# Expert matrices of a mixture layer loaded in rows of 4 KB instead of 2 KB

## The chip, the cores and the metric

The kernel runs on one core of a Trainium2 chip. The metric is the device time of one execution in microseconds (us). Before the change it was 2349.37 us, the median of three runs between 2348.11 and 2349.89 us. A number of loads or rows below is a count; 1 KB is 1024 bytes.

## The reference

Two blocks follow each other on 256 tokens of 1024 values, all in 32-bit floats. The first has two layers, and in its first layer 256 context tokens run beside. Each layer of it modulates and normalizes, attends (`mixer_ab`, then `mixer_c`), and ends in a mixture of 32 experts, of which each token takes two. The second block (two more layers of other attention and a dense feed-forward part) is not touched by the change. What matters here is the mixture:

```
h = rms_norm(x, norm_ffn[l]) * (1 + scale) + shift
pg = softmax(h @ w_group + b_group); le = h @ w_expert + b_expert    # group, then two experts of its eight
expert_block = lambda xb, e: (silu(xb @ w1[e]) * (xb @ w3[e])) @ w2[e]  # w1, w3: 1024 x 512; w2: 512 x 1024
out[token] = sum over its two experts of weight * expert_block(h[token], e)
```

One expert matrix is 2 MB, so a layer reads 32 x 3 x 2 MB = 192 MB (201.3 million bytes) of expert weights, whatever the tokens choose.

## The kernel before

One program runs on five engines: TensorE (PE) multiplies, VectorE (DVE) and ScalarE (ACT) work on rows, GpSimd (POOL) does small pieces, and SyncE (SP) issues nearly all loads. A scheduler of the compiler orders most instructions; `late` (line 185) and the order tokens on TensorE (`pe`, line 1019) hold the loads and the mixture's products in the order of the text.

The mixture (`moe`, line 997) takes the experts in 16 pairs. The two experts of a pair work side by side on TensorE, each on 64 of the 128 columns, so 64 token slots each. `up` (line 1225) multiplies the gathered inputs `xp` by `w1` and `w3` of a pair, k from 0 to 7 over the 1024 input values. `turn` transposes the hidden values to `gp`, and `down` (line 1253), one pair behind, multiplies by `w2`, k from 0 to 3 over the 512 hidden values, first for output columns 0 to 511 (n = 0), then for 512 to 1023. `weigh` scales its result `y`, `scatter` adds it to the tokens every second pair, and `gather` makes the inputs `xp` for the next two pairs out of a one-hot matrix `G` and the normalized tokens, which line 1035 splits in two parts `hi` and `lo`. In the first layer `gather` and `scatter` run over 512 tokens (NT = 4 tiles of 128), in the second over 256 (NT = 2).

Each load of an expert matrix brings 512 KB into one slot of 128 partitions x 1024 values, by `raws` (line 295). For `w1` and `w3` that is two blocks of 128 rows of 512 values: partition p gets row p of the one block and row p of the next. For `w2` it is two blocks of 128 half rows of 512 values. Either way a partition receives two runs of 2 KB from two places in memory:

```
in_=ap[k0 * P:(k0 + g) * P, :].rearrange("(k p) f -> p k f", p=P)     # g = 1024 // cols = 2
ws = self.raws([ew("w2", e)[:, n * 512:n * 512 + 512] for e in es_])   # once for each n
```

A layer has 384 such loads and 22 slots (first layer) or 31 slots (second); `slots` and the table `MJ` (line 84) say which memory they use and when. A slot is filled again when the products that read it are done. The names `raw`, `r`, `x`, `y`, `wh` and `wl` in the rows are such slots. The 96 loads of `w_mod` in the first attention part (`mod_group`, line 362, the first 16 of them ahead of everything else) also bring 512 KB each, but as one run of 4 KB per partition: 1024 neighbouring columns of one row.

At the start `setup` (line 136) loads constants, biases and norms as short rows, transposes them into columns (`colA`), and loads the tokens `x`; its temporary memory is used again by the first slots.

Of the kernel before, what the change touches and what calls it, by code (L numbers as in the profile page):

```python
# [8 lines left out]
F32 = mybir.dt.float32  # L9
# [3 lines left out]
AF = mybir.ActivationFunctionType  # L13
ALU = mybir.AluOpType
# [104 lines left out]
class Kern:  # L119
# [16 lines left out]
    def setup(self, tmp):  # L136
        nc, I = self.nc, self.I
        kept = COFF["kept"][1]
        self.cst = self.t(self.cp, [P, kept])
        o3 = COFF["causal"][0]  # L140
        more = self.t(tmp, [P, CONST.shape[1] - o3])
        rows = self.t(tmp, [P, 2, P])
        rc = self.t(tmp, [16, P])
        nc.sync.dma_start(out=rc[0:8, :], in_=I["c"].rearrange("o (k p) -> (o k) p", p=P))
        nc.sync.dma_start(out=rc[8:16, :], in_=I["c_ctx"].rearrange("(k p) -> k p", p=P))
        nc.scalar.dma_start(out=self.cst, in_=I["const"][:, 0:kept])
        nc.scalar.dma_start(out=more, in_=I["const"][:, o3:])
        nc.scalar.dma_start(out=rows[0:96, 0, :], in_=I["b_mod"].rearrange("l (k p) -> (l k) p", p=P))
        nc.scalar.dma_start(out=rows[96:112, 0, :], in_=I["norm_mix"].rearrange("l (k p) -> (l k) p", p=P))
        nc.scalar.dma_start(out=rows[112:128, 0, :], in_=I["norm_ffn"].rearrange("l (k p) -> (l k) p", p=P))  # L150
        self.x = [self.res(4 + i) for i in range(4)]
        for i in range(4):
            src = I["x"][0] if i < 2 else I["ctx"][0]
            nc.scalar.dma_start(out=self.x[i], in_=src[(i % 2) * P:(i % 2 + 1) * P, :])
        self.ident = self.c("ident")
        self.colC = self.t(self.cp, [P, 16])
        tp = self.P("tp")
        nc.tensor.transpose(tp[:, 0:16], rc, self.ident[:16, :16])
        nc.vector.tensor_copy(self.colC, tp[:, 0:16])
        self.colA = self.t(self.cp, [P, P])  # L160
        tp = self.P("tp")
        nc.tensor.transpose(tp[:, 0:P], rows[:, 0, :], self.ident)
        nc.vector.tensor_copy(self.colA, tp[:, 0:P])
        more = {nm: more[:, COFF[nm][0] - o3:COFF[nm][0] - o3 + P] for nm in ("causal", "anti", "tri")}
        self.ones = self.t(self.cp, [P, 1])
        nc.vector.memset(self.ones, 1.0)
        self.identb = self.t(self.cp, [P, P], BF)
        nc.vector.tensor_copy(self.identb, self.ident)
        self.causb4 = self.t(self.cp, [P, 4, P], BF)
        nc.vector.tensor_copy(self.causb4, more["causal"][:, None, :].to_broadcast([P, 4, P]))  # L170
        self.causb = self.causb4[:, 0]
        self.antib = self.t(self.cp, [P, P], BF)
        nc.vector.tensor_copy(self.antib, more["anti"])
        self.mhalf = self.c("mhalf")
        self.trib = self.t(self.cp, [P, P], BF)
        nc.vector.tensor_copy(self.trib, more["tri"])
        self.onesb = self.t(self.cp, [P, P], BF)
        nc.vector.memset(self.onesb, 1.0)
        self.rank = self.c("rank")
        self.modcol = self.t(self.cp, [P, 2, 48, 2])  # L180
        self.modA = self.t(self.cp, [P, 2, 2, KT, 2])

    def late(self, **kw):

        self.tc.keep_in_program_order(self.nc.sync.dma_start(**kw))

    def setup_small(self):

        nc, I = self.nc, self.I
        self.wr = self.t(self.cp, [P, 2, KT, 36])  # L190
        self.br = self.t(self.cp, [P, 2, 36])
        for l in range(2):
            self.late(out=self.wr[:, l, :, 0:4], in_=I["w_group"][l].rearrange("(k p) f -> p k f", p=P))
            self.late(out=self.wr[:, l, :, 4:36], in_=I["w_expert"][l].rearrange("(k p) f -> p k f", p=P))
            self.late(out=self.br[:, l, 0:4], in_=I["b_group"][l:l + 1, :].to_broadcast([P, 4]))
            self.late(out=self.br[:, l, 4:36], in_=I["b_expert"][l:l + 1, :].to_broadcast([P, 32]))

# [94 lines left out]
        pool, tag, bufs = e  # L292
        return self.t(pool, [P, 1024], dt, tag=tag, bufs=bufs)

    def raws(self, aps):

        nk, cols = aps[0].shape[0] // P, aps[0].shape[1]
        g = 1024 // cols
        out = [[] for _ in aps]
        for k0 in range(0, nk, g):  # L300
            for o, ap in zip(out, aps):
                raw = self.slot("raw", F32)
                self.late(out=raw.rearrange("p (k f) -> p k f", k=g),
                                       in_=ap[k0 * P:(k0 + g) * P, :].rearrange("(k p) f -> p k f", p=P))
                o += [raw[:, i * cols:(i + 1) * cols] for i in range(g)]
        return out

# [54 lines left out]
    def mod_group(self, l, q, tag):  # L362


        nc = self.nc
        acc = self.P(tag)[:, 0:512]
        for step in range(4):
            hf = step // 2
            for k in range(4 * (step % 2), 4 * (step % 2) + 4):
                c0 = 2048 * q + 1024 * hf  # L370
                w = self.raws([self.I["w_mod"][l][k * P:k * P + P, c0:c0 + 1024]])[0][0]
                for c in range(4):
                    m = nc.tensor.matmul(acc[32 * c:32 * c + 32, 256 * hf:256 * hf + 256], self.csf[:, k, :],
                                         w[:, 256 * c:256 * c + 256], start=(k == 0), stop=(k == KT - 1))
                    self.tc.stamp_issue_order_token(m.ins, "mod")
            if step < 3:
                yield
        m = self.slot("wh", F32)[:, 0:512]
        nc.scalar.activation(m, acc, AF.Copy)
        tp = self.P("tp")  # L380
        for j in range(4):
            nc.tensor.transpose(tp[:, j * P:(j + 1) * P], m[:, j * P:(j + 1) * P], self.ident)

        for hf in range(2):
            tv = tp[:, 256 * hf:256 * hf + 256].rearrange("p (j c s) -> p c j s", j=2, c=4)[:, :, :, 0:2]
            b0 = q * 16 + 8 * hf
            bias = self.colA[:, l * 48 + b0:l * 48 + b0 + 8].rearrange("p (c j) -> p c j", c=4)
            nc.vector.tensor_tensor(out=self.modcol[:, l, b0:b0 + 8, :].rearrange("p (c j) s -> p c j s", c=4), in0=tv,
                                    in1=bias[:, :, :, None].to_broadcast([P, 4, 2, 2]), op=ALU.add)
        if q != 1:  # L390
            which = q // 2
            g = self.colA[:, 96 + 16 * which + 8 * l:96 + 16 * which + 8 * l + 8]
            sc = self.modcol[:, l, 24 * which + 8:24 * which + 16, :]
            nc.vector.scalar_tensor_tensor(self.modA[:, l, which], sc, 1.0, g[:, :, None].to_broadcast([P, KT, 2]),
                                           op0=ALU.add, op1=ALU.mult)
        yield
# [572 lines left out]
    def logits(self, l, who, xt, t, tag, half):  # L969
# [4 lines left out]
        for b in range(2):  # L974
# [1 line left out]
            nc.scalar.activation(half(), xt[:, c], AF.Square, accum_out=ss[:, b:b + 1])  # L976
            tp = self.P("tp")
            for j in range(4):
                nc.tensor.transpose(tp[:, j * P:(j + 1) * P], xt[:, (4 * b + j) * P:(4 * b + j + 1) * P], self.ident)
            xT = half()  # L980
            if b == 0:
                nc.scalar.activation(xT, tp, AF.Copy)
# [14 lines left out]
    def moe(self, l, whos, ahead=list):  # L997
# [37 lines left out]
        xp_ = []  # L1035
        for i, x in enumerate(xs):
            hi, lo = (self.t(mp, [P, D], F32R) for _ in range(2))
            nc.scalar.activation(hi, x, AF.Copy, scale=rr_[:, i:i + 1])
            stt(lo, x, rr_[:, i:i + 1], hi.bitcast(F32), op0=ALU.mult, op1=ALU.subtract)
            xp_.append((hi, lo))  # L1040
        st = lambda *s, dt=F32, **kw: self.t(mp, [P, NT] + list(s), dt, **kw)
        big_ = lambda: self.t(mp, [P, 160], tag="big", bufs=1)
# [182 lines left out]
        def up(es_, xp, between=()):  # L1225
# [4 lines left out]
            for b, nm in enumerate(("w1", "w3")):  # L1230
                if b and between:
                    scatter(between)
                ws = self.raws([ew(nm, e) for e in es_])
                for k in range(KT):
                    for i, w in enumerate(ws):
                        c = slice(64 * i, 64 * i + 64)
                        mm(H[c, b, :], xp[:, k, c], w[k], start=(k == 0), stop=(k == KT - 1))
# [14 lines left out]

        def down(es_, gp):
            y = self.P("mm").rearrange("p (a b) -> p a b", a=2)
            for n in range(2):
                ws = self.raws([ew("w2", e)[:, n * 512:n * 512 + 512] for e in es_])
                for k in range(4):
                    for i, w in enumerate(ws):
                        c = slice(64 * i, 64 * i + 64)
                        mm(y[c, n, :], gp[:, k, c], w[k], start=(k == 0), stop=(k == 3))  # L1260
            return y[:64 * len(es_)]

        def weigh(y, tk, w):
# [701 lines left out]
```

## Time and profile before

| | |
|---|---|
| median of the runs | 2349.37 us |
| the profiled execution, its own time | 2353.45 us |
| its span, to which the rows refer | 2351.7 us |
| PE busy | 2181.2 us (93%) |
| DVE, ACT, POOL busy | 1119.8, 780.7, 345.9 us |
| bytes moved by DMA | 593.12 MB, 252 GB/s over the span |
| mixture of the first layer, about | 345 to 870 us |
| mixture of the second layer, about | 1119 to 1648 us |

The span is what lies between the first and the last instruction; the time of the run has 1.75 us around it. A busy PE counts a product from its start to its modelled end, with its place in the pipeline, so 93% does not say that TensorE had no time left. The DMA share can exceed 1, as neighbouring packets overlap a little in the records.

### The profile page before, as it was taken

How to read it: one execution, taken by the hardware profiler on the slowest of the kernel's cores; microseconds unless marked ns; L12 is line 12 of the kernel's file. 1: busy time of each engine (PE TensorE's matmuls, PEld its weight loads, DVE VectorE, ACT ScalarE, POOL GpSimd, SP SyncE). 2: the span in 40 equal slices, each digit the busy share in tenths (PEclk: the TensorE clock that was granted, in tenths of full speed). 3: DMA queues.
4: the chain of work that ended last, by engine and by line, in shares of the span. 5: the costliest groups of instructions: out<-in, count | busy, mean ns of one | idle time of the engine just before them, and what ended most of it. 6: DMA issues, size and time to landing. Idle time of an engine off the chain costs nothing. (4 is left out here: it accounts for less than half of the span.)

```text
span 2351.7 us, 32726 instructions
## 1 busy us (share of the span) xinstructions
PE 2181.2 (93%) x12405; PEld 1391.2 (59%) x12405; DVE 1119.8 (48%) x2251; ACT 780.7 (33%) x1585; POOL 345.9 (15%) x478
## 2 busy tenths in 40 slices
PE   5999989999999998998899999999899999899998
PEld 3865564444444437986433333333667998767997
DVE  4565664434343347766312122221566654666654
ACT  3444542111111115655201110110555443655443
POOL 1621120000000003443000000000323110232111
PEclk8999999999999999999899999999989999989999
DMA  8467639999999983220999999999433652425561
GB/s 290 134 226 270 220 113 367 381 387 387 387 387 386 387 303 114 77 72 9 357 387 387 386 387 387 386 387 383 152 126 116 230 178 99 160 84 169 188 207 37
DMA packets 306785, 593.12 MB, mean 252 GB/s; under 512 B 25270, under 2 KB 57020, under 8 KB 306620
## 3 DMA queue, kind: packets, MB, share of 16 engines
q1 hardware_dynamic: 305436, 587.68, 70.3%
q10 hardware_dynamic: 1184, 3.27, 0.4%
q8 instruction: 100, 1.64, 0.3%
q14 instruction: 65, 0.53, 0.1%
HBM read 589.82 MB, written 1.05 MB: 251 GB/s over the span
## 5 line engine op out<-in xcount | busy, mean ns | idle before, releaser
L330 POOL TENSOR_TENSOR wl<-raw,wh 128x1024 fp32r<-128x1024 f32 (+1 forms) x17 | 41.4, 2439 | 1148.8 <-SPq L1325 529.7
L1239 ACT ACTIVATE hs<-mm 128x512 f32<-128x512 f32 x32 | 19.1, 597 | 501.4 <-PE mm L1024 501.4
L330 DVE TENSOR_TENSOR wl<-raw,wh 128x1024 fp32r<-128x1024 f32 (+3 forms) x113 | 145.1, 1292 | 47.8 <-ACT wh L327 47.5
L1240 DVE TENSOR_TENSOR hs<-mm,hs 128x512 f32<-128x512 f32 x32 | 22.1, 691 | 297.6 <-ACT hs L1239 297.5
L1024 PE MATMUL mm<-x,xp 128*64 128x512 f32 x476 | 157.0, 601 | 4.7 <-DMA x<-in_w_dram 4.6
L1024 PE MATMUL mm<-raw,xp 128*64 128x512 f32 x464 | 149.4, 600 | 4.0 <-DMA raw<-in_w_dram 3.9
L327 ACT ACTIVATE wh<-raw 128x1024 fp32r<-128x1024 f32 (+3 forms) x113 | 115.8, 1032 | 84.2 <-PE pa L351 23.6
L1024 PE MATMUL mm<-r,xp 128*64 128x512 f32 x400 | 137.0, 601 | 4.1 <-DMA r<-in_w_dram 4.1
L1295 DVE TENSOR_TENSOR r<-tp,r 128x512 f32<-128x512 f32 x96 | 66.1, 690 | 102.3 <-PE tp L1024 102.1
L1250 ACT ACTIVATE gp<-tp 128x512 f32<-128x512 f32 x32 | 19.1, 597 | 264.4 <-PE tp L1248 264.4
L1024 PEld LDWEIGHTS tp<-G,u 128*128 128x128 f32 x768 | 97.7, 199 | 8.5 <-issue 8.5
L1024 PE MATMUL tp<-G,u 128*128 128x256 f32 x768 | 99.9, 292 | 2.7 <-DVE G L1129 2.7
L1024 PE MATMUL mm<-y,xp 128*64 128x512 f32 x264 | 98.4, 602 | 3.7 <-DMA y<-in_w_dram 3.6
L1024 PE MATMUL tp<-ys,GT 128*128 128x512 f32 x384 | 95.5, 402 | 6.4 <-DVE ys L1281 4.5
L349 PE MATMUL pa<-wh,u 128*128 128x256 f32 x320 | 92.7, 292 | 3.2 <-ACT ac L836 2.9
L351 PE MATMUL pa<-wh,u 128*128 128x256 f32 x320 | 92.7, 291 | 1.1 <-DVE u L345 1.1
L1024 PEld LDWEIGHTS tp<-ys,GT 128*128 128x128 f32 x384 | 71.4, 190 | 36.7 <-issue 13.0
L350 PE MATMUL pa<-wl,u 128*128 128x256 f32 x320 | 92.2, 289 | 0.2 <-DVE wl L330 0.2
L1882 PE MATMUL o<-u,xwl 128*128 128x256 f32 x320 | 90.7, 284 | 0.4 <-DVE xwl L330 0.4
L1024 PEld LDWEIGHTS mm<-x,xp 128*64 128x64 f32 x476 | 44.2, 136 | 79.1 <-issue 47.1
L1880 PE MATMUL o<-u,xwh 128*128 128x256 f32 x320 | 91.0, 285 | 0.0
L1881 PE MATMUL o<-u,xwh 128*128 128x256 f32 x320 | 90.8, 285 | 0.0
(516 smaller groups left out, 5463.8 us busy)
## 6 DMA issues: line engine op xcount, KB each, us to landing
raw<-in_w_dram SPq DMA_DIRECT2D x179, 512.0 KB, 10.8
x<-in_w_dram SPq DMA_DIRECT2D x172, 512.0 KB, 10.8
r<-in_w_dram SPq DMA_DIRECT2D x147, 512.0 KB, 10.8
y<-in_w_dram SPq DMA_DIRECT2D x96, 512.0 KB, 10.8
wh<-in_w_dram SPq DMA_DIRECT2D x87, 512.0 KB, 10.8
wl<-in_w_dram SPq DMA_DIRECT2D x87, 512.0 KB, 10.8
raw<-in_w_mod_dram SPq DMA_DIRECT2D x84, 512.0 KB, 5.6
xraw<-in_w_ff_dram SPq DMA_DIRECT2D x68, 512.0 KB, 4.5
```

The lines of the kernel that those rows point to most:

```text
L327: nc.scalar.activation(wh, raw, AF.Copy)
L330: (nc.vector if lo == "v" else nc.gpsimd).tensor_tensor(out=wl, in0=raw, in1=wh.bitcast(F32), op=ALU.subtract)
L349: mm(o, xh, wh, start=start, stop=False)
L350: mm(o, xh, wl, start=False, stop=False)
L351: mm(o, xl, wh, start=False, stop=stop)
L1024: mm = lambda *a, **kw: pe(nc.tensor.matmul(*a, **kw))
L1239: nc.scalar.activation(sg_, H[:r, 0], AF.Silu)
L1240: tt_(out=sg_, in0=H[:r, 1], in1=sg_, op=ALU.mult)
L1295: tt_(out=x, in0=o, in1=x, op=ALU.add)
L1880: mm(p1[:, j, :], wh[:, c], h[:, k, :], start=(k == 0), stop=False)
L1881: mm(p1[:, j, :], wh[:, c], lo[:, k, :], start=False, stop=False)
L1882: mm(p1[:, j, :], wl[:, c], h[:, k, :], start=False, stop=(k == KT - 1))
```

## The change

Three things change in the mixture. `raws` takes the order of rows as an argument, and `up` asks for "(p k) f -> p k f": partition p now gets rows 2p and 2p + 1 of a block of 256, which lie beside each other in memory. So the k-th slice of a matrix no longer holds rows 128k to 128k + 127, but the even or the odd rows of a block. `down` loads whole rows of `w2` (1024 values, one block of 128 rows per load) and turns its loops round: k outside, n inside. The number of loads, their bytes, and their slots stay as they were.

All that meets the up matrices is reordered to fit: the tokens' transposes for the router (`logits`), the router's weights (`setup_small`, two loads with a stride where there was one), the columns of shift, scale and norm (`mod_group` transposes a strided view in some places, `setup` loads three more short pieces, transposes them twice and copies them over), and the split of the tokens into `hi` and `lo`, which reads every second value and writes runs of 128, in two instructions where there was one.

```
+        rows2 = self.t(tmp, [24, 256])
...
+        nc.scalar.dma_start(out=rows2[0:8, :], in_=I["b_mod"][0, 3072:5120].rearrange("(g x) -> g x", x=256))
+        nc.scalar.dma_start(out=rows2[8:16, :], in_=I["b_mod"][1, 3072:5120].rearrange("(g x) -> g x", x=256))
+        nc.scalar.dma_start(out=rows2[16:24, :], in_=I["norm_ffn"].rearrange("l (g x) -> (l g) x", x=256))
...
+        for j in range(2):
+            nc.tensor.transpose(tp[:, j], self.two(rows2, 1)[:, 0, j], self.ident[:24, :24])
+        nc.vector.tensor_copy(self.colA[:, 0:96].rearrange("p (l g j) -> p l g j", l=2, j=2)[:, :, 12:20],
+                              tp[:, :, 0:16].rearrange("p j (l g) -> p l g j", l=2))
+        nc.vector.tensor_copy(self.colA[:, 112:128].rearrange("p (m j) -> p m j", j=2), tp[:, :, 16:24].rearrange("p j m -> p m j"))
...
+    def two(a, g):
+        return a.rearrange("r (g p j) -> r g j p", g=g, j=2)
...
-            self.late(out=self.wr[:, l, :, 4:36], in_=I["w_expert"][l].rearrange("(k p) f -> p k f", p=P))
+                for j in range(2):
+                    self.late(out=self.wr[:, l, j::2, c], in_=I[nm][l].rearrange("(g p j) f -> p g j f", p=P, j=2)[:, :, j])
...
-    def raws(self, aps):
+    def raws(self, aps, rows="(k p) f -> p k f"):
...
-                                       in_=ap[k0 * P:(k0 + g) * P, :].rearrange("(k p) f -> p k f", p=P))
+                          in_=ap[k0 * P:(k0 + g) * P, :].rearrange(rows, p=P))
...
-                nc.tensor.transpose(tp[:, j * P:(j + 1) * P], xt[:, (4 * b + j) * P:(4 * b + j + 1) * P], self.ident)
+                nc.tensor.transpose(tp[:, j * P:(j + 1) * P], self.two(xt, 4)[:, 2 * b + j // 2, j % 2], self.ident)
...
-            nc.scalar.activation(hi, x, AF.Copy, scale=rr_[:, i:i + 1])
-            stt(lo, x, rr_[:, i:i + 1], hi.bitcast(F32), op0=ALU.mult, op1=ALU.subtract)
+            hv, lv = (a.rearrange("r (g j p) -> r g j p", g=4, j=2) for a in (hi, lo))
+            for j in range(2):
+                src, h = self.two(x, 4)[:, :, j], hv[:, :, j]
+                nc.scalar.activation(h, src, AF.Copy, scale=rr_[:, i:i + 1])
+                stt(lv[:, :, j], src, rr_[:, i:i + 1], h.bitcast(F32), op0=ALU.mult, op1=ALU.subtract)
...
-                ws = self.raws([ew(nm, e) for e in es_])
+                ws = self.raws([ew(nm, e) for e in es_], "(p k) f -> p k f")
...
-            for n in range(2):
-                ws = self.raws([ew("w2", e)[:, n * 512:n * 512 + 512] for e in es_])
-                for k in range(4):
+            ws = self.raws([ew("w2", e) for e in es_])
+            for k in range(4):
+                for n in range(2):
                     for i, w in enumerate(ws):
                         c = slice(64 * i, 64 * i + 64)
-                        mm(y[c, n, :], gp[:, k, c], w[k], start=(k == 0), stop=(k == 3))
+                        mm(y[c, n, :], gp[:, k, c], w[k][:, n * 512:n * 512 + 512], start=(k == 0), stop=(k == 3))
```

On SP the loads stand at the same places in both programs; here is the passage of the first layer in which the loads of `w3` of one pair are followed by those of `w2` of the pair before (the last numbers are partitions x elements, and a form of three numbers has two runs per partition). Before:

```order
L185 DMA raw_1155_4656<-in_w3_dram 128x2x512
L185 DMA raw_1156_4658<-in_w3_dram 128x2x512
L185 DMA raw_1159_4680<-in_w2_dram 128x2x512
L185 DMA r3_1160_4682<-in_w2_dram 128x2x512
L185 DMA raw_1161_4684<-in_w2_dram 128x2x512
```

The same passage after:

```order
L201 DMA raw_1157_4677<-in_w3_dram 128x1024
L201 DMA raw_1158_4679<-in_w3_dram 128x1024
L201 DMA raw_1161_4701<-in_w2_dram 128x1024
L201 DMA r3_1162_4703<-in_w2_dram 128x1024
L201 DMA raw_1163_4705<-in_w2_dram 128x1024
```

Nothing moved there; each of the 768 loads is one run of 1024 values per partition instead of two of 512.

On ACT, at the very start, the queue of short loads ahead of the tokens grows. Before:

```order
L149 DMA u_4_75<-in_norm_mix_dram 16x128
L150 DMA u_4_75<-in_norm_ffn_dram 16x128
L154 DMA r4_6_84<-in_x_dram 128x1024
L154 DMA r5_7_85<-in_x_dram 128x1024
L154 DMA r6_8_86<-in_ctx_dram 128x1024
```

After:

```order
L150 DMA u_4_75<-in_norm_mix_dram 16x128
L151 DMA u_4_75<-in_norm_ffn_dram 16x128
L152 DMA u_5_76<-in_b_mod_dram 8x256
L153 DMA u_5_76<-in_b_mod_dram 8x256
L154 DMA u_5_76<-in_norm_ffn_dram 8x256
L158 DMA r4_7_88<-in_x_dram 128x1024
```

Three issues were put ahead of the loads of the tokens and of ACT's first computation. In the attention parts the scheduler also exchanges neighbouring products, and a few products of `mod_group` stand earlier or later among them; their number is the same.

## Rows read from the trace of the kernel before

**Rows 1.** The page's 40 slices: mean DMA share in tenths, and GB/s.

```profile
DMA  8467639999999983220999999999433652425561
GB/s 290 134 226 270 220 113 367 381 387 387 387 387 386 387 303 114 77 72 9 357 387 387 386 387 387 386 387 383 152 126 116 230 178 99 160 84 169 188 207 37
```

**Rows 2.** Stretches: length, busy time of engines (instructions), granted clock, DMA share, GB/s.

```profile
480.00:540.00 60.00, 59.25 (x286) 28.16 (x284) 25.51 (x50) 8.95 (x17) 0.00 (x0) 1.00 1.05 387
1080.00:1140.00 60.00, 45.34 (x248) 36.21 (x248) 39.98 (x115) 21.66 (x51) 10.35 (x19) 0.83 0.32 119
```

**Rows 3.** DMA queue, 500 to 600 us: packets, MB, share of 16 engines.

```profile
q1 hardware_dynamic: 20005, 38.57, 104.9%
```

**Rows 4.** The same queue, 12 to 28 us.

```profile
q1 hardware_dynamic: 1809, 6.59, 102.4%
```

**Rows 5.** Instructions in time, PE, 14 to 22 us: start, length, line, tiles, idle before.

```profile
17.60 1.08 PE L373 MATMUL f<-x,u 128*32 128x256 f32 x8 [0.20 <-DMA x<-in_w_mod_dram]
18.88 1.08 PE L373 MATMUL f<-x,u 128*32 128x256 f32 x8 [0.20 <-DMA x<-in_w_mod_dram]
```

**Rows 6.** The same view, second layer's mixture.

```profile
1630.18 1.93 PE L1024 MATMUL mm<-y,gp 128*64 128x512 f32 x6 [0.28 <-DMA y<-in_w_dram]
1632.88 2.44 PE L1024 MATMUL mm<-x,gp 128*64 128x512 f32 x8 [0.28 <-DMA x<-in_w_dram]
```

**Rows 7.** Waits of the SP queue: us in total, times, longest.

```profile
SPq L185 <- DMA raw<-in_w_dram: 121.8, 165, 1.0
```

**Rows 8.** Instructions in time, PE, first layer's mixture: three gathers and a scatter.

```profile
405.40 7.82 PE L1024 MATMUL tp<-G,u 128*128 128x256 f32 x64
463.95 7.82 PE L1024 MATMUL tp<-G,u 128*128 128x256 f32 x64
...
576.78 7.55 PE L1024 MATMUL tp<-ys,GT 128*128 128x512 f32 x32
...
722.29 7.82 PE L1024 MATMUL tp<-G,u 128*128 128x256 f32 x64
```

**Rows 9.** The same, second layer's mixture: a scatter and a gather.

```profile
1288.12 3.92 PE L1024 MATMUL tp<-ys,GT 128*128 128x512 f32 x16
1298.98 4.10 PE L1024 MATMUL tp<-G,u 128*128 128x256 f32 x32
```

**Rows 10.** Instructions in time, SP, start of the first layer's mixture.

```profile
357.70 3.98 SPq L185 DMA_DIRECT2D wl<-in_w_dram  x3
370.35 2.08 SPq L185 DMA_DIRECT2D r<-in_w_dram  x3
```

**Rows 11.** Instructions in time, all engines, 0 to 14 us.

```profile
2.56 0.44 ACTq L150 DMA_DIRECT2D u<-in_norm_ffn_dram  x1
...
6.87 0.18 DVE L360 COPY u<-u 128x16 f32<-128x16 f32 x1 [0.50 <-ACT u L357]
7.12 6.96 SPq L185 DMA_DIRECT2D x<-in_w_mod_dram  x9
```

**Rows 12.** Lines: instructions, ns shortest/median/longest, first and last start, form.

```profile
L1039 DVE SCALAR_TENSOR_TENSOR u<-r,rr,u x6: 1270/1272/1285, 340.2 to 1121.3; 128x1024 fp32r<-128x1024 f32 x6
...
L1276 DVE SCALAR_TENSOR_TENSOR gs<-u,ow,u x32: 745/752/2757, 396.7 to 874.9; 128x512 f32<-128x512 f32 x32
```

**Rows 13.** Groups by line and form, DVE, 335 to 360 us: busy, mean ns.

```profile
L1087 DVE TENSOR_TENSOR u<-u,u 128x128 f32<-128x128 f32 x2 | 0.6, 289 | 0.0
...
L1062 DVE TENSOR_TENSOR big<-lg,u 128x128 f32<-128x128 f32 x1 | 0.4, 377 | 0.0
```

**Rows 14.** Instructions in time, end of the second layer's mixture.

```profile
1638.85 4.10 PE L1024 MATMUL mm<-raw,gp 128*64 128x512 f32 x16 [0.75 <-ACT gp L1250]
...
1649.04 0.75 DVE L1279 SCALAR_TENSOR_TENSOR gs<-mm,sl,u 128x512 f32<-128x512 f32 x1 [6.83 <-PE mm L1024]
```

**Rows 15.** Stretch of the first attention part, columns as in Rows 2.

```profile
60.00:345.00 285.00, 275.84 (x2098) 190.73 (x2099) 163.69 (x416) 139.43 (x328) 90.00 (x134) 0.99 0.57 190
```

**Rows 16.** Stretch of 1 us, second block's feed-forward part: PE busy, clock, DMA share, GB/s.

```profile
1870.00:1871.00 1.00, 1.00 (x6) 1.00 1.02 410
```

More of the change, by code (lines that the diff above doesn't have):

```diff
@@ L163, in setup @@
         nc.vector.tensor_copy(self.colA, tp[:, 0:P])
+        tp = self.P("tp")[:, 0:48].rearrange("p (j m) -> p j m", j=2)
+        for j in range(2):
[3 more added lines that the diff above has]
+        nc.vector.tensor_copy(self.colA[:, 112:128].rearrange("p (m j) -> p m j", j=2), tp[:, :, 16:24].rearrange("p j m -> p m j"))
         more = {nm: more[:, COFF[nm][0] - o3:COFF[nm][0] - o3 + P] for nm in ("causal", "anti", "tri")}
@@ L181, in setup @@
         self.modA = self.t(self.cp, [P, 2, 2, KT, 2])
+    @staticmethod
+    def two(a, g):
+        return a.rearrange("r (g p j) -> r g j p", g=g, j=2)
     def late(self, **kw):
@@ L192, in setup_small @@
         for l in range(2):
-            self.late(out=self.wr[:, l, :, 0:4], in_=I["w_group"][l].rearrange("(k p) f -> p k f", p=P))
-            self.late(out=self.wr[:, l, :, 4:36], in_=I["w_expert"][l].rearrange("(k p) f -> p k f", p=P))
+            for c, nm in ((slice(0, 4), "w_group"), (slice(4, 36), "w_expert")):
+                for j in range(2):
+                    self.late(out=self.wr[:, l, j::2, c], in_=I[nm][l].rearrange("(g p j) f -> p g j f", p=P, j=2)[:, :, j])
             self.late(out=self.br[:, l, 0:4], in_=I["b_group"][l:l + 1, :].to_broadcast([P, 4]))
@@ L381, in mod_group @@
         for j in range(4):
-            nc.tensor.transpose(tp[:, j * P:(j + 1) * P], m[:, j * P:(j + 1) * P], self.ident)
+            src = m[:, j * P:(j + 1) * P]
+            if 24 <= 16 * q + 8 * (j // 2) < 40:
+                src = self.two(m, 2)[:, j // 2, j % 2]
+            nc.tensor.transpose(tp[:, j * P:(j + 1) * P], src, self.ident)
         for hf in range(2):
```

## The prediction, made before the run

> **What bounds the kernel now.** I began with the page's 40 slices [rows 1]: the DMA engines are nearly full in two plateaus, slices 7 to 14 and 20 to 28, at 381 to 387 GB/s. These are the two mixtures. A rate that stays on one number for hundreds of microseconds is a ceiling, so the second view was the waits of the SP queue [rows 7]: before a load is issued, SP waits for an earlier load to land, 165 times for the slots called `raw` alone and for 1.0 us at most. The queue is held by the DMA engines' pace and not by slots. From 500 to 600 us each packet of at most 2 KB keeps an engine for 16 x 100 x 1.049 / 20005 = 0.084 us [rows 3]. A load of 524,288 bytes at 387 GB/s takes 1.355 us. In the second layer TensorE works at just that pace: two products start 2.70 us apart, two loads each, and both had waited for a load [rows 6]. That layer is bound by DMA to its end.
>
> In the first layer TensorE has more to do, and I had to see which of the two ends last. Two gathers, one period of two expert pairs (48 loads) apart, lie 58.55 us apart at first; over the next four periods it is (722.29 - 463.95) / 4 = 64.6 us [rows 8]. 48 loads at 1.355 us are 65.0 us. So TensorE needs 58.55 us for a period when nothing holds it; it starts late, works off its delay until soon after 464 us, and from there DMA is the bound here too. PE's 93% on the page does not show that.
>
> Outside the mixtures DMA is not the bound: in the first attention part TensorE is busy 275.8 of 285 us, at a DMA share of 0.57 [rows 15].
>
> **The load of 4 KB rows, the main term.** The trace holds loads of this very kind. From 12 to 28 us only `w_mod` loads are in flight, 512 KB each as one 4 KB run per partition. They bring 6.59 MB in 16 us, 412 GB/s [rows 4], and TensorE, which waits for each of them, starts 18.88 - 17.60 = 1.28 us apart [rows 5]. That is 0.075 us less per load than 1.355. The `w_mod` rows lie 24 KB apart in memory, the expert rows will lie back to back; in the feed-forward part, whose second matrices have whole rows of 4 KB back to back, a single microsecond reaches 410 GB/s [rows 16]. I take 1.28 us. The ends are 1.355 (nothing gained) and 1.273 us (the 412 GB/s).
>
> How many loads profit? In the first layer the 22 slots fill before the first product: SP issues three loads from 357.70 us and then none until 370.35 us [rows 10]. Those 22 gain nothing, as the products wait for the router and not for them. The other 362 do: 362 x 0.075 = 27.2 us. In the second layer 31 slots outlast the start, so all 384 count: 28.8 us.
>
> Does TensorE allow it? 48 loads at 1.28 us are 61.4 us, still above the 58.55 us [rows 8], so DMA stays the bound. The margin shrinks from 6.5 to 2.9 us per period, so TensorE needs about twice as long to work off its late start; until then the slots are full and DMA stands still now and then. From 370 to 405 us a faster DMA brings 27.3 loads instead of 25.8; the 1.5 loads more find no slot, and that time, 1.5 x 1.28 = 2 us, is lost. By the gather at 722.29 us some 260 loads are through, 19.5 us saved; TensorE alone could have saved 4 x (64.6 - 58.55) = 24 us there. In the second layer the scatter takes 3.92 and the gather 4.10 us instead of 7.55 and 7.82 [rows 8, 9], so its period needs 58.55 - 3.6 - 3.7 = 51.2 us, and nothing is near. First layer: 27.2 - 2 = 25 us; both: 54 us. Ends for the lost time: 0 and 6 us.
>
> **The other parts.** The inverted loops of `down` keep the number of products, weight loads and loads. The first half of `y` was not read early before: for the last pair its 16 products start at 1638.85 us and last 4.10 us, but VectorE reads the first half only at 1649.04 us, after the last product of the second half [rows 14]. So it costs nothing that both halves now end together.
>
> At the start ACT issues three more loads ahead of the tokens and of its own first instruction. An issue takes 0.44 us; the first `w_mod` load, at 7.12 us, follows a VectorE copy that waited for ACT [rows 11]. This chain moves by 3 x 0.44 = 1.3 us, and with it the 16 loads that TensorE waits for [rows 5]. Behind the waiting load on SP stand all loads of the first part. I take 1.3 us. If the DMA engines, still bringing in the tokens, cover it, it is 0; if the two new transposes and copies come late as well, 3 us.
>
> The split into `hi` and `lo` has twice the instructions, half as long. On VectorE one of 1024 values takes 1.272 us, one of 512 takes 0.752 us [rows 12]: 2 x 0.752 - 1.272 = 0.23 us for each of four tiles, 0.9 us in the first layer, in order ahead of the router's steps and so ahead of the first product. In the second layer the loads run on meanwhile, as its 31 slots are not full by then, and nothing is lost. No row shows a long read of every second value; a 128-value one with a stride took 377 ns instead of 289 [rows 13], 0.09 us per 128 values, at most 8 x 4 x 0.09 = 2.8 us more. I take 0.9 us; ends 0 and 3.7.
>
> Four more issues of router weights fall where TensorE has other work, the strided transposes keep their number, and the scheduler's exchanges in the attention parts move no work. TensorE's idle time from 60 to 345 us is 9.2 us [rows 15]; I take 0, with 5 us to either side.
>
> **Sum.** 25 + 28.8 - 1.3 - 0.9 = 51.6 us. The profiled execution took 2353.45 us around a span of 2351.7; its sum is 2353.45 - 51.6 = 2301.9 us. It was 4.1 us above the median of the runs, so against 2349.37 the forecast is **2298 us**. All terms at their good end: 746 x 0.082 + 5 = 66 us gained, 2283. With 1.28 us and all others at the bad end: 56 - 6 - 3 - 3.7 - 5 = 38 us, 2311.
>
> **Rivals.** *Only part of the 0.075 us comes with the row.* The `w_mod` stretch differs in other ways too: TensorE reads little there, and nothing else is loaded. For this speaks that no long stretch of expert loads with 4 KB rows exists; against it, that in the mixtures the rate is the same 387 GB/s in the first layer's crowded periods and the second's emptier ones [rows 1, 2], so what TensorE does is not what holds it. Per packet an engine needs 16 x 16 x 1.024 / 1809 = 0.145 us with 3.6 KB on average [rows 4], 0.084 us with 1.9 KB [rows 3]: 25.1 against 23.0 bytes per ns. With half of it: 28 us, less 3 us of costs: 2324 us.
>
> The Trainium skill speaks for this rival (DMA: Bandwidth & Descriptors, section "Why small descriptors are slow (HBM only)"): a packet pays a fixed 3 cycles or so beside one cycle per 32 bytes. An estimate by that page: two packets of 2 KB are 2 x 67 cycles, one of 4 KB 131, a gain of 2.2% or 0.03 us per load, 22.6 us in all and 2330 us. The trace shows 5.5% between its two kinds of load, and where they differ I go by the trace.
>
> *No gain at all.* The long run could be cut into 2 KB pieces by the queue, or the expert rows, back to back, could meet another limit of memory. Then only the costs remain: 2349.4 + 2.2 = 2352 us. Against it: `w_mod` loads have the same form, 128 x 1024, and show the large packets [rows 4], and [rows 16] shows back-to-back rows at 410 GB/s.
>
> The same page's table "Specifications" has a rule for this one: 512 bytes or more suffice for the line rate, so 2 KB rows would already be there. By it the time is that of this rival, 2352 us; 1.28 against 1.355 us speaks against it.
>
> *Slower: the granted clock.* Denser products in the first mixture could bring TensorE down from the full level of 2.4 GHz for part of the time. Its mean there is 1.00 now [rows 2]; at the 0.83 of the stretch before the second mixture [rows 2] a period is 58.55 / 0.83 = 70.5 us against 65.0, over 362 / 48 = 7.5 periods 41 us lost. The second layer, 51.2 / 0.83 = 61.7 us per period, would still gain 26 us. Result 2349 + 41 - 26 + 2 = 2366 us. It decides from where the first layer loses more than 26.4 us, a period of 68.5 us, which is a mean clock of 0.855. Against it: from 60 to 345 us TensorE is as dense, at 0.99 [rows 15].
>
> **Chances.** Forecast, 2287 to 2316 us: 0.78. Part of the rate: 0.09. No gain: 0.06. Slower: 0.04. The remaining 0.03 are larger gains. What this kernel's measurement can tell from no change is about 0.2%, 4.7 us. Faster: 0.78 + 0.09 + 0.03, less 0.01 for mishaps in the attention parts, 0.89; same 0.06; slower 0.05. The range from 2287 to 2319 us holds the forecast and the near end of the partial gain.
>
> **What would show it.** Right: 768 x 128 = 98,304 packets fewer on the SP queue (128 per expert load instead of 256); plateaus of 408 to 413 GB/s; products of the second layer 2.56 us apart where they were 2.70; gathers of the first layer 61.4 us apart; first `w_mod` load near 8.4 us. Wrong: plateaus at 387 to 400 GB/s; gathers at 58.6 us (TensorE the bound) or above 65; a granted clock below 0.95 in the first mixture; an attention part longer by over 5 us.

## The result and the profile after

The changed kernel takes 2290.25 us (median of four runs, 2288.74 to 2295.89) against 2349.63 us (2348.11 to 2350.84): a ratio of 0.9752, with a 95% interval of 0.9735 to 0.9769. Forecast were 2298 us, range 2287 to 2319. The profiled execution took 2290.15 us with a span of 2288.3; before it was 2353.45 and 2351.7.

The page's 40 slices after, the mean DMA share in tenths and GB/s, answer to [rows 1]:

```profile
DMA  8467639999999973220999999998525561615551
GB/s 290 137 225 261 224 112 370 399 409 409 409 409 409 409 283 119 80 70 10 390 409 409 409 409 409 409 409 318 185 70 181 192 205 62 204 47 190 197 193 38
```

Both plateaus stand at 409 where they stood at 387; between them nothing looks different. The SP queue has 207,196 packets where it had 305,436: 98,240 fewer, beside the forecast 98,304. Stretches after, with PE's busy time (instructions), granted clock, DMA share and GB/s, answer to [rows 2] and [rows 15]:

```profile
360.00:370.00 10.00, 10.00 (x68) 0.99 0.66 256
370.00:380.00 10.00, 10.00 (x51) 1.00 0.98 352
410.00:420.00 10.00, 10.00 (x50) 1.00 0.95 346
450.00:550.00 100.00, 100.00 (x521) 1.00 1.03 409
1200.00:1300.00 100.00, 95.90 (x397) 1.00 1.03 409
60.00:345.00 285.00, 273.76 (x2098) 1.00 0.58 194
```

At 409 GB/s a load of 524,288 bytes takes 1.282 us (1.28 forecast). The clock is 1.00, the full level of 2.4 GHz, in the stretches of both mixtures (0.99 from 360 to 370 us). Early in the first one (360 to 380, 410 to 420 us) the rate is still low: there the slots are full, and the DMA engines stand still now and then. SP's waits for products to release a slot, from 370 to 460 us (us in total, times, longest), show it:

```profile
SPq L201 <- PE mm L1044: 26.5, 24, 5.9
```

From 450 to 550 us TensorE is busy without a gap: it works off its late start out of filled slots. The DMA engines move their full 409 GB/s beside it, so this stretch, too, brings the end of the mixture nearer at the pace of the loads.

The DMA queue after, 450 to 550 us: packets, MB, share of 16 engines, to set beside [rows 3]:

```profile
q1 hardware_dynamic: 11213, 40.83, 102.5%
```

More bytes come in little more than half the packets; each now keeps an engine for 16 x 100 x 1.025 / 11213 = 0.146 us, where it was 0.084. SP's longest waits for a landed load after are still short, as in [rows 7]:

```profile
SPq L201 <- DMA raw<-in_w_dram: 145.3, 164, 1.4
```

The products of the second layer after, start and length in us, answer to [rows 6]:

```profile
1217.38 0.64 PE L1044 MATMUL mm<-raw,xp 128*64 128x512 f32 x1 [0.22 <-DMA raw<-in_w_dram]
...
1219.94 2.35 PE L1044 MATMUL mm<-raw,xp 128*64 128x512 f32 x8 [0.21 <-DMA raw<-in_w_dram]
1222.50 0.64 PE L1044 MATMUL mm<-r,xp 128*64 128x512 f32 x1 [0.21 <-DMA r<-in_w_dram]
```

They start 2.56 us apart, two loads each, and still wait for a load each time. The gathers of this layer keep that pace of DMA to the end: from 1196.87 to 1505.54 us they lie 61.4 to 62.5 us apart. The gathers of the first layer after answer to [rows 8] (here and below, rows between them are left out):

```profile
401.19 7.82 PE L1044 MATMUL tp<-G,u 128*128 128x256 f32 x64
459.73 7.82 PE L1044 MATMUL tp<-G,u 128*128 128x256 f32 x64
518.27 7.82 PE L1044 MATMUL tp<-G,u 128*128 128x256 f32 x64
577.91 7.82 PE L1044 MATMUL tp<-G,u 128*128 128x256 f32 x64
639.30 7.84 PE L1044 MATMUL tp<-G,u 128*128 128x256 f32 x64
701.97 7.82 PE L1044 MATMUL tp<-G,u 128*128 128x256 f32 x64
763.56 7.82 PE L1044 MATMUL tp<-G,u 128*128 128x256 f32 x64
```

The steps are 58.54, 58.54, 59.64, 61.39, 62.67 and 61.59 us. Two periods run at TensorE's own pace, one lies between, and from 578 us on it is the pace of DMA, 48 x 1.282 = 61.5 us. Before, DMA took over from the second period on.

Where the time came from, by stages of the two traces (a mixture from the issue that opens its stream of loads, to the start of its last scatter, us; in the first layer five loads are out some 40 us before):

```
                         before   after   difference
attention, to mixture 1   345.2   341.8      -3.4
mixture 1                 526.0   499.5     -26.5
attention 2               248.4   247.0      -1.4
mixture 2                 529.4   499.9     -29.5
second block              702.8   700.1      -2.7
span                     2351.7  2288.3     -63.4
```

### The profile page after: what moved, and what is told of

The parts are those of the page before. It is cut to its first block, busy times and chain, and to the rows that moved or that the text cites. A ratio compares the mean times of both kernels' runs of the same rounds, so it can differ in the third digit from the quotient of the medians.

```text
span 2288.3 us, 32754 instructions
## 1 busy us (share of the span) xinstructions
PE 2134.6 (93%) x12407; PEld 1380.8 (60%) x12407; DVE 1118.8 (49%) x2259; ACT 782.8 (34%) x1591; POOL 344.8 (15%) x478
## 3 DMA queue, kind: packets, MB, share of 16 engines
q1 hardware_dynamic: 207196, 587.68, 68.4%
q8 instruction: 100, 1.64, 0.3%
HBM read 589.85 MB, written 1.05 MB: 258 GB/s over the span
## 5 line engine op out<-in xcount | busy, mean ns | idle before, releaser
L1044 PE MATMUL mm<-x,xp 128*64 128x512 f32 x476 | 150.6, 599 | 1.9 <-DMA x<-in_w_dram 1.8
L1909 POOL TENSOR_TENSOR w<-w 128x512 f32<-128x512 f32 x32 | 46.7, 1459 | 281.2 <-DVE w L1907 281.2
```

The source lines that it names most:

```text
L1044: mm = lambda *a, **kw: pe(nc.tensor.matmul(*a, **kw))
L1909: nc.gpsimd.tensor_tensor(out=q, in0=r, in1=r, op=ALU.mult)
```

## The experiments

My theory: the length of the run that a partition receives sets the rate of the DMA engines, a packet per run, with a fixed price for each packet; the reordering, the inverted loops and the start cost next to nothing. Rivals: the reordering gave part of the gain; one matrix kind alone gave it; or the speed of the `w_mod` loads came from something else than their run.

**Four parts of the change.** The kernel before with the down matrices in whole rows:

```
-            for n in range(2):
-                ws = self.raws([ew("w2", e)[:, n * 512:n * 512 + 512] for e in es_])
-                for k in range(4):
+            ws = self.raws([ew("w2", e) for e in es_])
+            for k in range(4):
+                for n in range(2):
...
```

> The kernel before with whole rows of the down matrix alone; the up matrices stay in runs of 2 KB. If a load costs 1.355 us in two runs per partition and 1.282 us in one (the 387 and 409 GB/s of the two kernels), the 256 down loads of the two layers save 256 x 0.073 = 18.7 us: 2331 us, and two expert pairs of the first layer's later part take 32 x 1.355 + 16 x 1.282 = 63.9 us. Rival, the inverted loops of the down products are what helped (both halves of the result end together, other order of products): the whole saving of 59 us or most of it is here, below 2305 us. Rival, only long stretches of one kind of packet run at the higher rate: no gain, 2350 us.

Measured: 2331.02 us against 2346.66, ratio 0.9935 (0.9917 to 0.9954); gathers from 587 to 780 us lie 64.3 us apart on average. The changed kernel with that part undone, so the up matrices and the reordering alone:

> The changed kernel with the down matrices loaded as before, in half rows of 2 KB, and its old loops; the up matrices and all that is reordered for them as changed. By the price per load: 512 x 0.073 = 37.4 us less, some 1.5 us of it lost to full slots in the first layer; with the 7 us that the profiles differ by outside the mixtures if these belong to the reordering: 2306 us, without them 2313 us. Rival, loops of down: above 2330 us.

Measured: 2311.32 us, 0.9857 (0.9838 to 0.9876). The changed kernel with every run at 2 KB again, the down part undone and the order of rows in `up` too:

```
-                ws = self.raws([ew(nm, e) for e in es_], "(p k) f -> p k f")
+                ws = self.raws([ew(nm, e) for e in es_])
```

> The changed kernel with both kinds of expert loads put back to runs of 2 KB, but with all that reorders the inputs (the output is not the reference's, as the up matrices' rows no longer match their inputs). If the length of the runs is all: 387 GB/s in both mixtures, and 2350 us, or 2343 us if the 7 us outside the mixtures come from the reordering and what the scheduler makes of it. My forecast's costs of the reordering alone (1.3 us at the start, 0.9 us at the split) would give 2352 us. Rival, the reordering itself brought a good part of the gain: below 2335 us.

Measured: 2345.22 us, 0.9991 (0.998 to 1.0001). And the reverse, the kernel before with both kinds of long runs and the inverted loops, and no reordering:

> The kernel before with 4 KB runs for both kinds of expert matrices and the inverted down loops, and nothing reordered (the output is not the reference's, as inputs and rows of the up matrices don't match). If the runs are all: 409 GB/s in both mixtures and 2290 to 2297 us, the higher number if 7 us of the changed kernel's gain came from the reordering. Rival, the reordering: above 2310 us.

Measured: 2293.00 us, 0.9777 (0.9759 to 0.9794). From 480 to 600 us, columns as above, in the order in which they were told:

```profile
480.00:600.00 120.00, 118.72 (x578) 1.00 1.04 394
```

```profile
480.00:600.00 120.00, 119.38 (x590) 1.00 1.04 401
```

```profile
480.00:600.00 120.00, 117.93 (x564) 1.00 1.05 387
```

```profile
480.00:600.00 120.00, 119.95 (x606) 1.00 1.03 409
```

One third of the loads lengthened gives 394 GB/s, two thirds 401, none 387, all 409: by time per byte a mixture of the two kinds (1 / (1/3/409 + 2/3/387) = 394, and 401.4 the other way round). The gains, 15.6 and 35.3 us, stand near one third and two thirds of the 53.7 us of both together. Without long runs the reordering changes nothing that can be told from zero. What remains between long runs alone (0.9777) and the whole change (0.9752) lies within the two intervals.

The traces show it closer than the totals, with the stages cut as in the table of the result (us, one execution each):

```
                                  mixture 1   mixture 2   all else
before                              526.0       529.4      1296.3
down matrices long                  515.9       519.2      1293.4
up matrices long, reordered         508.8       510.6      1285.9
reordered, every run 2 KB           526.1       529.9      1290.2
both long, nothing reordered        500.1       500.3      1288.7
the whole change                    499.5       499.9      1288.9
```

The mixtures gain 20.4 us by the down matrices, 36.0 by the up matrices and 56.0 by both. Without the reordering both give 55.0, and the reordering alone gives nothing (-0.6). By the price of 0.073 us per load, 256 and 512 loads are worth 18.7 and 37.4 us.

**Shorter runs.** The kernel before with all 768 loads in four runs of 1 KB per partition:

```
+                    r0, c0 = 512 * (k0 // 4), 256 * (k0 // 2 % 2)
+                    self.late(out=raw.rearrange("p (k f) -> p k f", k=4),
+                              in_=ap[r0:r0 + 512, c0:c0 + 256].rearrange("(k p) f -> p k f", p=P))
```

> The kernel before with the same 768 expert loads of 512 KB, each in four runs of 1 KB per partition instead of two of 2 KB (four blocks of 128 quarter rows; the output is not the reference's, as products meet other rows). If a packet costs a fixed time and a time per byte, the two lengths measured so far give them: 0.0847 us an engine for 2 KB (1.355 us x 16 / 256) and 0.160 us for 4 KB (1.282 x 16 / 128), so 0.0377 us per KB and 0.0093 us fixed; a load in 512 packets then takes 1.50 us, 349 GB/s, and the kernel 746 x 0.147 = 110 us more than before, 2457 us. If the fixed part is the 3 cycles beside 32 for each KB that the Trainium skill's page gives (DMA: Bandwidth & Descriptors, Why small descriptors are slow), an estimate by that page is 70 against 67 cycles per 2 KB, 4.5% more: 1.416 us a load, 2392 us. If 2 KB and less run alike and only whole 4 KB packets are faster: 2347 us.

Measured: 2463.4 us, ratio 1.0492 (1.0461 to 1.0522). The same two kinds of stretch in its trace:

```profile
450.00:550.00 100.00, 95.85 (x452) 1.00 1.10 348
1250.00:1400.00 150.00, 137.36 (x511) 1.00 1.10 348
```

348 GB/s in both, whatever TensorE does. The fixed price per packet holds on the other side too (2457 us expected). That runs of 2 KB and less are alike (2347 us) does not hold. Nor does the estimate by the Trainium skill (DMA: Bandwidth & Descriptors, "Why small descriptors are slow (HBM only)"), 2392 us.

**The streams by themselves.** A kernel that does nothing but load, 24 MB in each of nine parts:

> A program that only streams weights from memory into slots (it computes nothing of the reference and writes zeros), in nine parts of 24 MB each, one behind the other: loads of 512 KB in runs of 2 KB, 4 KB, 4 KB with the rows 24 KB apart, 1 KB, 512 bytes; loads of 1 MB in runs of 2 KB, then 8 KB; loads of 2 MB in runs of 16 KB; 2 KB again. With the run length alone as cause: 387, 409, 409, 349, and 290 GB/s; then 387 (the size of a load does nothing), and, by the same fixed and byte parts, 8 x 1024 / (0.0093 + 8 x 0.0377) ns x 16 engines = 422 GB/s and 428 GB/s. If what TensorE and the other engines do beside held the rate in the kernels, the parts are faster here than there. If the distance of the rows matters, the third part differs from the second. If the size of a load matters, the sixth part is above 387 GB/s.

Stretches inside the nine parts (length, busy times, clock, DMA share, GB/s), in the order of the expectation:

```profile
32.00:60.00 28.00, 0.00 (x0) 0.00 (x0) 1.00 1.05 387
80.00:120.00 40.00, 0.00 (x0) 0.00 (x0) 1.00 1.03 410
140.00:180.00 40.00, 0.00 (x0) 0.00 (x0) 1.00 1.03 410
205.00:250.00 45.00, 0.00 (x0) 0.00 (x0) 1.00 1.10 348
275.00:335.00 60.00, 0.00 (x0) 0.00 (x0) 1.00 1.20 290
358.00:395.00 37.00, 0.00 (x0) 0.00 (x0) 1.00 1.05 387
420.00:445.00 25.00, 0.00 (x0) 0.00 (x0) 1.00 1.01 422
475.00:510.00 35.00, 0.00 (x0) 0.00 (x0) 1.00 1.01 431
545.00:590.00 45.00, 0.00 (x0) 0.00 (x0) 1.00 1.05 387
```

Every number is that of the kernels with the same run, with no engine at work. Rows 24 KB apart (third line) move as fast as rows back to back (second). Loads twice as large with the run unchanged (sixth) gain nothing; the same size with a run of 8 KB (seventh) does. So it is the run, and not the load's size, the place of the rows or the other engines. Time on an engine for one run is 16 x bytes / rate: 28.2 ns for 512 bytes, 47.1 for 1 KB, 84.7 for 2 KB, 159.8 for 4 KB, 310.6 for 8 KB. Each doubling adds the same 37.6 ns per KB, and about 9.4 ns stay fixed. The last stretch is short against its loads of 2 MB, so its 431 is rough (428 expected).

**What TensorE would need.** The changed kernel without the loads of `w3`:

```
-                ws = self.raws([ew(nm, e) for e in es_], "(p k) f -> p k f")
+                if not b:
+                    ws = self.raws([ew(nm, e) for e in es_], "(p k) f -> p k f")
```

> The changed kernel without its loads of w3: the second product of each up step reads the slots of w1 again, so the output is not the reference's; products, gathers and scatters stay. A period of two pairs has 32 loads, 41 us at 1.282 us each. If the loads alone bound both mixtures and TensorE needs 58.55 us (first layer) and 51.2 us (second) for a period, as the prediction worked out, all gathers of the first layer lie 58.5 us apart and those of the second 51.2 us. The first layer gets about 14 us shorter (763.56 - 356.32 = 407 us from first to last gather in the changed kernel, 44.9 + 6 x 58.54 = 396 without waits, and one more period), the second about 60 (483 us of products against 8 x 51.2 + some 12 at the end): 2290 - 74 = 2216 us, 2200 to 2230. Rival, that something else holds the products (a product that reads memory while DMA writes it, a weight load): gathers stay near 61 and 58 us or more, and the time above 2260 us.

Measured: 2190.07 us, ratio 0.9323 (0.9304 to 0.9342). Its gathers, of the first layer and then of the second:

```profile
578.59 7.82 PE L1044 MATMUL tp<-G,u 128*128 128x256 f32 x64
637.14 7.82 PE L1044 MATMUL tp<-G,u 128*128 128x256 f32 x64
695.68 7.82 PE L1044 MATMUL tp<-G,u 128*128 128x256 f32 x64
...
1272.55 4.10 PE L1044 MATMUL tp<-G,u 128*128 128x256 f32 x32
1323.40 4.10 PE L1044 MATMUL tp<-G,u 128*128 128x256 f32 x32
1374.27 4.10 PE L1044 MATMUL tp<-G,u 128*128 128x256 f32 x32
```

58.55 and 50.86 us apart to the end, where 58.55 and 51.2 had been worked out: nothing but the loads held the products. The total was expected 26 us too high. The first mixture gained 15.4 us (14 expected), the second 78.4 instead of 60. There I had added 12 us for the end to eight periods that already held it (410 us from the first gather to the last scatter, 8 x 51.2 = 410), and had put 483 us for the same stretch of the changed kernel, which takes 489 there. The other 6.8 us are differences of the stages outside, in one execution.

**A version with longer runs.** The changed kernel, and in the second layer `w2` in 64 loads of 1 MB with runs of 8 KB, in four slots made of two each (the rest of the edit makes those slots):

```
+            srcs = [ap[256 * g:256 * g + 256, :].rearrange("(p j) f -> p j f", j=2) for ap in aps]
+            if self.rings.get("wide"):
+                for o, src in zip(out, srcs):
+                    raw = self.slot("wide", F32)
+                    self.late(out=raw.rearrange("p (j f) -> p j f", j=2), in_=src)
...
-                pe(nc.tensor.transpose(tp[:, f, 0:r], sg_[:, f * P:(f + 1) * P], self.ident[:r, :r]))
+                pe(nc.tensor.transpose(tp[:, f, 0:r], self.two(sg_, 2)[:, f // 2, f % 2], self.ident[:r, :r]))
```

> The changed kernel, and in the second layer the down matrices in loads of 1 MB with one run of 8 KB per partition (two neighbouring rows), into four slots of twice the width; the hidden values are transposed in the matching order, everywhere. 128 loads of 512 KB become 64 of 1 MB. The stream of 8 KB runs measured by itself moved 422 GB/s against 409: 1.242 us per 512 KB instead of 1.282, 0.040 us x 128 = 5.1 us less. The coarser last loads may cost 0.5 to 2 us at the end. Forecast 2286 us against 2290 for the changed kernel, ratio to before near 0.973; plateau of the second layer 413 GB/s; packets of the SP queue 8,192 fewer than 207,196. Rival, that the four wide slots are released too late and SP waits: second layer longer, 2292 to 2300 us, with waits of TensorE for DMA above 1 us. Rival, that nothing is gained inside the kernel: 2290 us and 409 GB/s.

Measured: 2288.62 us (2282.78 to 2292.07), ratio to before 0.9744 (0.9724 to 0.9763). A stretch of its second mixture:

```profile
1200.00:1300.00 100.00, 91.69 (x390) 1.00 1.02 413
```

The rate is the expected 413, and the second mixture takes 496.2 us instead of 499.9. The SP queue has 197,980 packets, 9,216 fewer, where 8,192 were expected. The times of the two versions overlap, so it is not shown to be faster than the changed kernel: 3.7 us in the trace are less than their runs can tell.

## Why the prediction was right, point by point

*The bound, and 1.28 us per load.* Right in kind and size: 1.282 us. "Not by slots" was too much, though: beside the waits of [rows 7] SP waited 194 times, 125.8 us in all, for products to release a slot, and between 370 and 460 us up to 8.6 us at a time. That is the early part of the first layer, for which the forecast itself counts full slots; later in the two mixtures, from 560 us on, none of these waits is longer than 1.1 us, and the rate stays at 387 GB/s. What the forecast left open, whether the speed of the `w_mod` loads belongs to their rows, the streams settle: their 24 KB pitch and the idle engines make no difference. The choice to go by rows of the trace and against two rules of the Trainium skill (DMA: Bandwidth & Descriptors) was what made the number. The runs show a fixed part of 9.4 ns for each run of bytes, and 290 GB/s for runs of 512 bytes against 422 for runs of 8 KB. By the Trainium skill's section "Why small descriptors are slow (HBM only)" a packet pays some 3 cycles beside one for 32 bytes, by its "Specifications" at 850 MHz; 9.4 ns would be 8 such cycles. By "Specifications" 512 bytes suffice for the line rate, and 290 against 422 GB/s says otherwise. The ceiling that the same section gives, 435 GB/s, agrees with the slope: 16 x 1024 bytes / 37.6 ns = 436.

*Second layer, 28.8 us.* Measured 29.5, and 29.1 with the long runs alone.

*First layer, 25 us less 0.9 for the split.* Measured 26.5, and 25.9 with the long runs alone. That TensorE takes longer to work off its late start, and that DMA takes over again from there, came as forecast; the gathers are 58.54 us apart for two periods before they reach the forecast 61.4. By the gather at 763.56 us the saving since the first load is (788.05 - 345.19) - (763.56 - 341.76) = 21.1 us, with 788.05 the same gather before. Some 308 loads were through by then (the forecast's 260 at the gather before, and 48), 23.1 us at 0.075 or 22.5 at the measured 0.073. So 1.4 to 2 us were lost to full slots, near the forecast's 2.

*Start, 1.3 us.* The mechanism came, its price did not. The start after, answering to [rows 11], and ACT's first copy of `mod_group`:

```profile
3.03 0.57 ACTq L152 DMA_DIRECT2D u<-in_b_mod_dram  x1
3.89 0.28 ACTq L153 DMA_DIRECT2D u<-in_b_mod_dram  x1
4.21 0.31 ACTq L154 DMA_DIRECT2D u<-in_norm_ffn_dram  x1
...
7.93 0.17 DVE L377 COPY u<-u 128x16 f32<-128x16 f32 x1 [1.23 <-ACT u L374]
8.18 5.84 SPq L201 DMA_DIRECT2D x<-in_w_mod_dram  x9
...
35.14 0.60 ACT L396 ACTIVATE wh<-f 128x512 f32<-128x512 f32 x1 [21.50 <-PE f L390]
```

That copy before:

```profile
35.36 0.60 ACT L379 ACTIVATE wh<-f 128x512 f32<-128x512 f32 x1 [21.65 <-PE f L373]
```

The three issues put ACT's next one off by 1.5 us (to 4.56 us from 3.03), and the first `w_mod` load is issued 1.06 us later, at 8.18. Yet TensorE's first product of such loads starts at 13.82 us, where it started at 13.87, and the copy behind the first 16 at 35.14, where it started at 35.36. So the good end of this term held: the forecast's own condition, DMA engines that still bring in the tokens, covers the delay. Between 7 and 9 us their share was 0.73 and 0.80 before, and is 0.96 and 0.99 after.

*The split, 0.9 us.* Its instructions after, answering to [rows 12], for VectorE two and for ACT four in a line:

```profile
336.97 2.74 ACT L1061 ACTIVATE u<-r,rr 128x512 fp32r<-128x512 f32 x4
...
340.22 2.97 ACT L1061 ACTIVATE u<-r,rr 128x512 fp32r<-128x512 f32 x4
```

```profile
338.95 1.82 DVE L1062 SCALAR_TENSOR_TENSOR u<-r,rr,u 128x512 fp32r<-128x512 f32 x2
...
341.45 1.40 DVE L1062 SCALAR_TENSOR_TENSOR u<-r,rr,u 128x512 fp32r<-128x512 f32 x2
...
342.94 1.40 DVE L1062 SCALAR_TENSOR_TENSOR u<-r,rr,u 128x512 fp32r<-128x512 f32 x2
```

On VectorE the first pair takes 1.82 us and each of the other three 1.40: 6.0 us for four tiles, where the four whole instructions took 5.1. That is the 0.9 us taken. A read of every second value costs nothing extra: 0.74 us for one instruction (median), where the 512 values of [rows 12] took 0.752. But no time was lost by it. Before, VectorE stood waiting 1.4 us among these steps (0.44 for POOL's `rr`, 0.93 for ACT). The first gather comes 20.1 us after VectorE's last `hl` of the attention part, where it came 20.7, and with runs of 2 KB the first mixture lasts 526.1 us reordered and 526.0 before.

*Inverted loops.* Forecast at 0; the kernel with long runs and the loops alone gains its 53.7 us and gives no sign of a price. Nor do the mixtures with down runs and loops alone: they gain 20.4 us, where the runs are worth 18.7. The loops by themselves were not run.

*Parts outside the mixtures, 0 within 5 us.* In the profiled executions this term was the furthest off: -3.4 (where +1.3 stood for the start), -1.4 and -2.7 us. It explains most of why 63.4 us were gained there and 51.6 forecast. By the medians 59.4 us were gained, and 2290.25 us lies 3 us above the low end of the range. Most of the term need not be the reordering's: all else than the mixtures takes 1288.7 us with long runs and nothing reordered and 1288.9 with the whole change, and the kernel before had 1296.3 in an execution 4 us above its median. The second block, which the change leaves as it was, lasts from 696.1 us (without `w3`) to 702.8 us (before) in the profiled executions.

One piece of it is the reordering's, with the other sign than the forecast's cost. SP issues the first mixture's stream of loads when POOL has made the last `rr` of the norm. Before:

```profile
343.53 1.63 POOL L421 TENSOR_TENSOR rr<-rsv,u 128x1 f32<-128x1 f32 x1
345.19 1.90 SPq L185 DMA_DIRECT2D x<-in_w_dram  x4
```

After:

```profile
341.19 0.55 POOL L441 TENSOR_TENSOR rr<-rsv,u 128x1 f32<-128x1 f32 x1
...
341.76 1.76 SPq L201 DMA_DIRECT2D x<-in_w_dram  x4
```

In the four kernels that are not reordered this `rr` takes 1.63 or 1.64 us, and the loads start 7.7 us after VectorE's last `hl` of the attention part (337.48 us before); in the five that are, it takes 0.55 us, and they start 5.5 us after it (336.25 us after). So the loads start 2.2 us earlier by the reordering. Why POOL is slow there without it is not shown; its long instruction stands beside one of VectorE's whole splits (343.49 us). In the total of the reordering's own run, 1.4 us less with an interval from 4.7 less to 0.2 more, 2.2 us cannot be told from zero.

*The rivals.* Part of the rate: 409 GB/s rules it out. No gain: ruled out by the same row. The granted clock: 1.00 in the stretches of both mixtures, and the first layer's periods at TensorE's own pace stayed at 58.54 us.

## What to carry to other kernels

When a stage sits on one DMA rate for hundreds of microseconds, look at the packets: here a run of bytes for one partition cost 9.4 ns and 37.6 ns per KB on its engine, so lengthening runs from 2 to 4 KB was worth 5.4% of the loading time and the next doubling would be worth 3%. A load of the same form elsewhere in the trace gave the new rate exactly; a period of work without waits gave the point at which the next engine takes over. Reordering what meets the data was nearly free here (within 0.2% of nothing), as it happens where the data is transposed or copied anyway. A small instruction of another engine that releases the first load can be worth a look as well: here it moved a stream of loads by 2.2 us.

## What was not expected of the hardware

The rate of a run length was the same to within 1 GB/s with all engines at work and with none: 348, 387 and 409 GB/s for 1, 2 and 4 KB in the kernels, 348, 387 and 410 alone. Doubling the load from 512 KB to 1 MB at the same run changed it by nothing. And the shares of DMA time in the records exceed 1 by more as runs get shorter (1.01 at 8 KB, 1.05 at 2 KB, 1.20 at 512 bytes), so a share above 1 is a sign of many small packets and not of more work done.
